# Seven products instead of eight for the up and gate projection of two segment groups

## The chip, the cores and the metric

One core of a Trainium2 chip runs the whole kernel. The metric is device time in microseconds (us): the median over several runs. The engines are PE (matrix multiply), DVE (vector), ACT (activation, scalar), POOL (GpSimd) and SP, which here only issues DMAs; each works off its own queue of instructions in order.

## The reference

One layer of a streaming encoder over 2192 tokens (8 requests of 16, 16 meta tokens, one prompt of 2048), width 1024. A first half mixes tokens (RWKV and mLSTM heads). The second half is a gated network with a causal convolution over three tokens:

```
D_MODEL = 1024
D_FF = 2816
FFN_CONV = 3
...
    x = x + jnp.concatenate([ya, yb], axis=-1).astype(x.dtype) @ w_out
    h2 = rmsnorm(x, norm_ffn)
    ug = h2 @ w_up
    u, fconv1 = causal_dwconv(ug[..., :D_FF], fconv0, ffn_conv_w, ffn_conv_b)
    x = x + (jax.nn.silu(u) * ug[..., D_FF:]) @ w_down
    return x, (shift1, S1, bconv1, C1, n1, m1, fconv1)
```

A last RMSNorm makes the outputs. All inputs and outputs are float32.

## The kernel before, in words

Activations lie with channels on the 128 partitions and tokens along the free axis. Tokens are cut into six segments, 0 to 5: segment 0 has 272, the others 384. A weight tile is 128 columns of a weight matrix against all eight blocks of 128 input channels.

Each factor of a large product is split into two parts that PE reads as fp32r: hi is a cast (ACT), lo is the source minus hi (DVE). `gemm` (L308 to L320) then runs three matmuls per block of 128 channels: hi by hi, hi by lo and lo by hi, all into one bank of PSUM. A product over 1024 channels is thus 24 matmuls.

`load_w` (L362 to L383) fetches a weight tile (512 KB) by SP's queue into a raw tile (2 of these), casts it on ACT (L374) and subtracts on DVE (L259), into one of four w tiles; a tile with a cache name is kept in DRAM in its two parts and comes again as 1 MB by POOL's queue. `split_acts` (L348 to L361) does the same for activations, two channel blocks (768 columns) at a time (L359, L360).

The first phase walks the six segments through the mixers, up to about 1880 us. At its end `ffn_acts` makes the split normed inputs (h2hi, h2lo) of segments 0 and 1.

The second phase is the gated network. The segments form three groups of two:

```
GROUPS = [[0, 1], [2, 3], [4, 5]]
CHUNKS = [(0, 5), (5, 10), (10, 14), (14, 18), (18, 22)]
```

For each group, the loop runs over chunks of f, a tile of 128 of the 2816 inner channels (22 in all). For each f, the u tile and the g tile of w_up are loaded, and `mm` computes u and g for both segments: 4 x 24 = 96 matmuls. Then u goes from PSUM to ub (ACT or DVE, L248 and L252), POOL puts the two tokens of the segment before at its front, DVE does the convolution in three steps (L1234, L1236 twice), ACT a tanh (L1238), DVE finishes the SiLU (L1239) and multiplies by g in PSUM (L1240); the result is split into gh (ACT, L1243) and gw (DVE and POOL in turn).

After each chunk, the down projection runs over eight output tiles d (`staggered`: the second segment one d behind the first), 3 matmuls per f, and DVE adds each bank to the residual x in SBUF (L1259). There are four residual tiles x2 (`mix`), so those of the next group load while a group still works. Ahead of the last down of a group, the inputs of the next group are made: `norm` scales x by the row's root mean square (broadcast by PE into ps_ch, L331; L1200) and splits it. For segment 5 the output projection of the mixers, `last_out`, is computed there too, ahead of the last down of the second group (L1189).

At the end of each group, squares are summed over channels (L1151 to L1155), over partitions on PE, the power is taken on POOL (L326, L327), PE broadcasts it, and DVE scales x for the output (L1266).

PSUM has eight banks under the tags gm (2), a, m, iv (2) and ch (2). A scheduler sets the order on each engine from the program's order and some places of preference (`ranked`); the engines' orders are then fixed. The pools cp, wp and big live over both phases.

Of the kernel before, what the change touches and what calls it, by code (L numbers as in the profile page):

```python
# [12 lines left out]
F32 = mybir.dt.float32  # L13
F32R = mybir.dt.float32r
AF = mybir.ActivationFunctionType
ALU = mybir.AluOpType
# [17 lines left out]
CHUNKS = [(0, 5), (5, 10), (10, 14), (14, 18), (18, 22)]  # L34
# [58 lines left out]
# Places in the scheduler's order, engines, PSUM rings and buffer counts of the stages.  # L93
# [118 lines left out]
def trunk_kernel(ctx: ExitStack, tc: tile.TileContext, A):  # L212
# [5 lines left out]
    def knob(name, default):  # L218
        """The first segment has its own choices, where there are any."""
# [4 lines left out]
    def rank(stage):  # L224
        """Instructions of a stage move by their knob's places in the scheduler's order of preference."""
# [40 lines left out]
    cst = cp.tile([128, CONST.shape[1]], F32, name="cst")  # L266
# [70 lines left out]
    def token_sums(pr, acc, n):  # L337
        """Sums over the channels, tokens on the partitions."""
# [9 lines left out]
    def split_acts(name, half, n, src=None, scale=None, raws=None):  # L348
        """float32r parts of an activation tile: src is loaded, scale(raw, k, j) fills or scales tile k in raw[:, j]."""
# [14 lines left out]
    def load_w(src, cache=None):  # L364
        """float32r parts of a weight tile; parts that come again are kept in DRAM."""
# [21 lines left out]
    def pt(tag, shape=(128, 512)):  # L387
        """A bank, in the shape asked for."""
# [6 lines left out]
    with ExitStack() as p1:  # L395
        pool = lambda n, b, **k: p1.enter_context(tc.tile_pool(name=n, bufs=b, **k))
        kp = pool("kp", 1)
# [53 lines left out]
        def build_h0():  # L451
            """The first segment's activations: squares are summed over the channels by ones on the tensor engine."""
# [50 lines left out]
        def shifted(w, h, s, ct, out):  # L503
            """Projected columns of tile ct, each mixed with the token before it."""
# [115 lines left out]
        def rwkv(u, s, ws, h, lo1, lo2):  # L620
# [157 lines left out]
            def chain():  # L778
# [4 lines left out]
                def sb(t, h):  # L783
                    """S' and the rank-one updates' left factors of head h."""
# [101 lines left out]
        def conv4(w, h, s, j, out):  # L886
            """Projected columns, causal conv of four taps and SiLU; j is the channel tile of q|k."""
# [142 lines left out]
        def out_proj(s, ds):  # L1030
            """Residual plus the projected mixers' output, kept in DRAM."""
# [23 lines left out]
        def ffn_acts(s):  # L1055
            """The normed input of the second half, for the segments that come first there."""
# [74 lines left out]
    with ExitStack() as p2:  # L1131
        pool = lambda n, b, **k: p2.enter_context(tc.tile_pool(name=n, bufs=b, **k))
        kp = pool("kp2", 1)
        accp = pool("acc", 4)
# [218 lines left out]
```

## Time and profile before

| | us |
|---|---|
| median of 3 runs | 3523.97 |
| lowest and highest run | 3508.24, 3531.34 |
| span of the profiled execution | 3507.6 |
| PE busy in this span | 3411.7 (97%) |
| DVE, ACT, POOL busy | 2146.4, 1152.2, 941.0 |

The profiled execution is one of its own; the page has its span, from the first to the last event on the core. The times of the runs are taken around the whole execution. A duration in the rows below is of this one execution; "busy" of a group of instructions counts overlapping ones once, so busy divided by the count is the distance between instructions that stand back to back, and the mean is that of a single one.

### The profile page before, as it was taken

How to read it: one execution, taken by the hardware profiler on the slowest of the kernel's cores; microseconds unless marked ns; L12 is line 12 of the kernel's file. 1: busy time of each engine (PE TensorE's matmuls, PEld its weight loads, DVE VectorE, ACT ScalarE, POOL GpSimd, SP SyncE). 2: the span in 40 equal slices, each digit the busy share in tenths (PEclk: the TensorE clock that was granted, in tenths of full speed). 3: DMA queues.
4: the chain of work that ended last, by engine and by line, in shares of the span. 5: the costliest groups of instructions: out<-in, count | busy, mean ns of one | idle time of the engine just before them, and what ended most of it. 6: DMA issues, size and time to landing. Idle time of an engine off the chain costs nothing.

```text
span 3507.6 us, 63114 instructions
## 1 busy us (share of the span) xinstructions
PE 3411.7 (97%) x24228; PEld 3123.6 (89%) x24228; DVE 2146.4 (61%) x5529; ACT 1152.2 (33%) x2826; POOL 941.0 (27%) x2294
## 2 busy tenths in 40 slices
PE   7999999999999999999989999999999999999998
PEld 6776888888888888888878999999999999999998
DVE  7777767666665776766665555574545447454544
ACT  5443444333433343343332222232222223222222
POOL 2532335434334444434421000021000012010002
PEclk9888999999999999999988999999999999999999
DMA  8753666455455545545523222232222233212221
GB/s 307 252 172 109 218 221 202 150 171 179 148 164 172 174 151 186 184 142 195 167 85 110 76 79 73 73 113 84 67 66 67 66 127 111 66 48 67 67 67 63
DMA packets 187565, 459.40 MB, mean 131 GB/s; under 512 B 68320, under 2 KB 111744, under 8 KB 156800
## 3 DMA queue, kind: packets, MB, share of 16 engines
q1 hardware_dynamic: 136648, 187.25, 18.0%
q0 software_dynamic: 28080, 204.48, 17.6%
q10 hardware_dynamic: 22536, 63.63, 4.8%
q8 instruction: 191, 3.13, 0.4%
q14 instruction: 110, 0.90, 0.1%
HBM read 381.68 MB, written 73.63 MB: 130 GB/s over the span
## 4 chain that ended last, share of the span: by engine, by line
PE 86%; DVE 6%; DMA 3%; ACT 2%; issue 1%; POOL 1%; ACTq 0%; SPq 0%; POOLq 0%; DVEq 0%
PE ps_gm L320 43%; PE ps_iv L320 11%; PE ps_a L320 10%; PE ps_m L320 5%; PE ps_iv L305 2%; PE ps_a L712 2%; PE ps_ch L826 1%; PE ps_ch L845 1%; PE ps_ch L839 1%; PE ps_iv L810 1%; PE ps_m L955 1%; DVE w L259 1%; DMA xt<-in_x_dram 1%; PE ps_a L305 1%; PE ps_m L972 1%
## 5 line engine op out<-in xcount | busy, mean ns | idle before, releaser
L320 PE MATMUL ps_gm<-hhi,w 128*128 128x384 f32 (+1 forms) x2976 | 813.1, 345 | 7.4 <-ACT w L374 2.2
L320 PE MATMUL ps_gm<-h2hi,w 128*128 128x384 f32 (+1 forms) x2816 | 701.1, 327 | 0.2 <-ACT ub L1221 0.2
L320 PEld LDWEIGHTS ps_gm<-hhi,w 128*128 128x128 f32 x2976 | 540.8, 193 | 30.2 <-issue 5.5
L320 PE MATMUL ps_gm<-hlo,w 128*128 128x384 f32 (+1 forms) x1488 | 502.2, 338 | 3.0 <-DVE hlo L360 3.0
L320 PEld LDWEIGHTS ps_gm<-h2hi,w 128*128 128x128 f32 x2816 | 500.0, 188 | 0.9 <-ACT ub L1221 0.5
L320 PE MATMUL ps_gm<-h2lo,w 128*128 128x384 f32 (+1 forms) x1408 | 459.9, 327 | 0.0
L374 ACT CAST w<-wraw 128x1024 fp32r<-128x1024 f32 (+2 forms) x291 | 259.4, 892 | 455.8 <-PE ps_iv L320 243.0
L320 PE MATMUL ps_iv<-gh,w 128*128 128x384 f32 (+1 forms) x1410 | 361.2, 330 | 0.0
L320 PE MATMUL ps_a<-h2hi,w 128*128 128x384 f32 (+1 forms) x1408 | 358.0, 327 | 0.0
L259 DVE TENSOR_TENSOR w<-wraw,w 128x1024 fp32r<-128x1024 f32 (+2 forms) x291 | 301.0, 1035 | 64.4 <-ACT w L374 60.4
L320 PEld LDWEIGHTS ps_gm<-hlo,w 128*128 128x128 f32 x1488 | 287.3, 193 | 9.5 <-DVE hlo L360 3.4
L320 PEld LDWEIGHTS ps_gm<-h2lo,w 128*128 128x128 f32 x1408 | 264.9, 188 | 0.0
L320 PEld LDWEIGHTS ps_iv<-gh,w 128*128 128x128 f32 x1410 | 252.5, 188 | 0.0
L320 PEld LDWEIGHTS ps_a<-h2hi,w 128*128 128x128 f32 x1408 | 251.0, 188 | 0.1
L320 PE MATMUL ps_iv<-gw,w 128*128 128x384 f32 (+1 forms) x705 | 232.6, 330 | 0.0
L320 PE MATMUL ps_a<-h2lo,w 128*128 128x384 f32 (+1 forms) x704 | 230.5, 327 | 0.0
L1238 ACT ACTIVATE fth<-ac 128x384 f32<-128x384 f32 (+1 forms) x132 | 67.2, 510 | 398.1 <-DVE ac L1236 388.7
L1231 POOL COPY h_f<-ub 128x2 f32<-128x2 f32 x88 | 16.4, 187 | 636.7 <-DVE ub L252 403.9
L320 PE MATMUL ps_m<-gh,w 128*128 128x384 f32 (+1 forms) x702 | 186.0, 330 | 0.0
L1259 DVE TENSOR_TENSOR x<-x,ps_iv 128x384 f32<-128x384 f32 (+1 forms) x160 | 85.3, 533 | 161.4 <-PE ps_iv L320 161.0
L1234 DVE TENSOR_SCALAR ac<-ub,d_fw,d_fb 128x384 f32<-128x384 f32 (+1 forms) x154 | 68.5, 457 | 182.8 <-ACT ub L248 157.1
L320 PE MATMUL ps_gm<-yhi,w 128*128 128x384 f32 (+1 forms) x640 | 168.3, 336 | 1.0 <-ACT yhi L359 0.7
(385 smaller groups left out, 6357.5 us busy)
## 6 DMA issues: line engine op xcount, KB each, us to landing
w<-wc POOLq DMA_DIRECT2D x155, 1024.0 KB, 5.4
wraw<-in_w_up_dram SPq DMA_DIRECT2D x132, 512.0 KB, 3.6
wc<-w ACTq DMA_DIRECT2D x31, 1024.0 KB, 6.5
wraw<-in_w_down_dram SPq DMA_DIRECT2D x72, 256.0 KB, 2.6
wraw<-in_w_in_dram SPq DMA_DIRECT2D x31, 512.0 KB, 5.9
wraw<-in_w_down_dram SPq DMA_DIRECT2D x48, 320.0 KB, 2.9
xraw<-in_xT_dram SPq DMA_DIRECT2D x36, 384.0 KB, 3.3
xt<-in_x_dram SPq DMA_DIRECT2D x15, 512.0 KB, 6.6
```

The source lines that it names most:

```text
L259: (V if e[turn[name] % len(e)] == "V" else G).tensor_tensor(out, a, b, op=op)
L305: T.matmul(out[h:h + 64], lhsT[h:h + 64], rhs[h:h + 64], start=start, stop=stop)
L320: T.matmul(ps, w, x, start=i == 0, stop=i == len(seq) - 1)
L374: S.copy(hi[:, :nk], raw[:, :nk])
L712: T.matmul(psS[hs, i, X], kb[hs, X, cl(c)], ar[hs, h, :, cl(c)], start=True, stop=True)
L810: T.matmul(pp[hs, i], TA[hs, 0, i], sb(SC[c][hs].unsqueeze(1), h)[:, 0], start=True, stop=True)
L826: T.matmul(pd[hs, :64], ar[:, h, x, cl(c)], vz[:, h], start=True, stop=x == 0)
L839: T.matmul(pz[hs, :64], kb2[:, h], vz[:, h], start=True, stop=True)
L845: T.matmul(py[hs, :64], sc[hs, 64:128], vz[hs, h], start=False, stop=True)
L1234: V.tensor_scalar(av, view(2), fwh[:, 44 + f:45 + f], fbh[:, f:f + 1], op0=ALU.mult, op1=ALU.add)
L1238: S.activation(th[:, :n], ac[:, :n], AF.Tanh)
L1259: V.tensor_tensor(X[s][:, d, :n], X[s][:, d, :n], p, op=ALU.add)
```

## The change

For the second and third group, u and g of both segments are computed as one product of 2 x 2 blocks by Strassen's scheme in Winograd's form. The left factor is [g; u] by two halves of the channels: A11 and A12 are the g tile's first and second four blocks, A21 and A22 those of the u tile. The right factor is the two halves of the channels (rows) by the two segments (columns): B11, B12, B21, B22. Seven products of half depth take the place of eight: 7 x 4 x 3 = 84 matmuls for 96. Its sums of weights are S1 = A21 + A22, S2 = S1 - A11, S3 = A11 - A21, S4 = A12 - S2; the sums of inputs are T1 to T4, made once per group (`ffn_parts`) with their hi and lo parts.

The products stay in three banks b1, b2, b3. Two are added in one bank by PE (start=False), and the sums that go to more than one output are taken by DVE from a bank read between two products (p1, u2, u3).

The first group is computed as before (`up_plain`). While it runs, it writes to DRAM: the two parts of each g tile (WG, 1 MB), of the second half of each u tile (WA, 0.5 MB), the raw sums S1 to S4 (WS, 1 MB; two sums on POOL, two on DVE) and the two parts of each down tile (WD). The other groups read these by SP's queue; the S tiles are split again on ACT and DVE in each group.

Further: the chunks are (0,3), (3,7), (7,11), (11,14), (14,17), (17,22); the down of a chunk stands behind the first f of the next chunk, and the finish of a group behind the first f of the next group. `last_out` moves into the first group, after the first chunk and one f more; its result is written to DRAM, like that of the other segments. There are two residual tiles instead of four, and the second phase has its own pool of weight tiles (wq: four w, three raw), which opens in the place of wp, a pool that now ends with the first phase. The convolution is an Identity on ACT with scale and bias, two steps on DVE, and a Silu on ACT. After the first group, `pinned` keeps the first matmul of each product in program order on PE.

The core of the diff:

```diff
-CHUNKS = [(0, 5), (5, 10), (10, 14), (14, 18), (18, 22)]
+CHUNKS = [(0, 3), (3, 7), (7, 11), (11, 14), (14, 17), (17, 22)]
...
-    wp = ctx.enter_context(tc.tile_pool(name="wp", bufs=1))
     big = ctx.enter_context(tc.tile_pool(name="big", bufs=2))
...
+    wp = p1.enter_context(tc.tile_pool(name="wp", bufs=1))
...
+        wq = pool("wq", 1)
-        accp = pool("acc", 4)
+        accp = pool("acc", 2)
...
+        quads = itertools.cycle([("gm", "iv", "a"), ("gm", "iv", "m")])
+        down_banks = itertools.cycle(("iv", "m", "iv", "a"))
...
+        def product(ps, w, x, start, stop):
+            for i, ((wh, wl), (xh, xl)) in enumerate(zip(w, x)):
+                for j, (l, r) in enumerate(((wh, xh), (wh, xl), (wl, xh))):
+                    ins = T.matmul(ps, l, r, start=start and i + j == 0, stop=stop and i == len(x) - 1 and j == 2, skip_group_check=not start)
+                    if pinned[0] and i + j == 0:
+                        tc.keep_in_program_order(ins)
...
+        def keep_sums(f, raw=None):
...
+            a11, a12, a21, a22 = raw["g"][:, 0:4], raw["g"][:, 4:8], raw["u"][:, 0:4], raw["u"][:, 4:8]
...
+            G.tensor_tensor(s1, a21, a22, op=ALU.add)
+            G.tensor_tensor(s3, a11, a21, op=ALU.subtract)
+            V.tensor_tensor(s2, s1, a11, op=ALU.subtract)
+            V.tensor_tensor(s4, a12, s2, op=ALU.subtract)
...
+        def conv(f, s, ub, ac):
...
+            for view, av in parts:
+                S.activation(av, view(2), AF.Identity, scale=PR("fw", 44 + f), bias=PR("fb", f))
+                for i in (1, 0):
+                    V.scalar_tensor_tensor(av, view(i), PR("fw", i * 22 + f), av, op0=ALU.mult, op1=ALU.add)
+            S.activation(ac[:, :n], ac[:, :n], AF.Silu)
...
+        def load_parts(f):
+            g = w_tile()
+            nc.sync.dma_start(f32(g), f32(WG[f][:]))
...
+            for i, names in enumerate((("S2", "S3"), ("S1", "S4"))):
+                raw = raw_tile()
+                nc.sync.dma_start(raw.rearrange("p (a k c) -> p a k c", a=2, c=128), WS[f][:, i])
+                t = w_tile()
+                split(t[:, 0], t[:, 1], raw.rearrange("p (k c) -> p k c", c=128))
...
+            a = w_tile()
+            nc.sync.dma_start(f32(a[:, :, 0:4]), f32(WA[f][:]))
...
+        def up_quad(f, segs, H, gl):
...
+            product(b1, W["A11"], H["B11"], True, True)
+            S.copy(p1, b1)
+            product(b2, W["S2"], H["T2"], True, True)
+            V.tensor_tensor(u2, b2, p1, op=ALU.add)
+            product(b1, W["A12"], H["B21"], False, True)
+            product(b2, W["S3"], H["T3"], False, True)
+            V.tensor_tensor(u3, b2, p1, op=ALU.add)
+            product(b3, W["S1"], H["T1"], True, True)
+            V.tensor_tensor(ub[1][:, 2:2 + n], b3, u3, op=ALU.add)
+            product(b2, W["A22"], H["T4"], False, True)
+            V.tensor_tensor(ub[0][:, 2:2 + n], b2, p1, op=ALU.add)
+            conv(f, segs[0], ub[0], ac[0])
+            V.tensor_tensor(ac[0], ac[0], b1, op=ALU.mult)
+            keep_gated(gl, f, segs[0], ac[0])
+            conv(f, segs[1], ub[1], ac[1])
+            product(b3, W["S4"], H["B22"], False, True)
+            V.tensor_tensor(u2, b3, u2, op=ALU.add)
+            V.tensor_tensor(ac[1], ac[1], u2, op=ALU.mult)
+            keep_gated(gl, f, segs[1], ac[1])
...
+        def ffn_parts(segs, rb):
...
+            for k in range(KD // 2):
...
+                    for i in range(2):
+                        V.scalar_tensor_tensor(r[:, i], r[:, i], PR("nf", j), rb[i], op0=ALU.mult, op1=ALU.mult)
...
+                pair(two[0], b2, ("B21", "B22"))
+                V.tensor_tensor(b1[:, 0], b1[:, 1], b1[:, 0], op=ALU.subtract)
+                V.tensor_tensor(b1[:, 1], b2[:, 1], b1[:, 1], op=ALU.subtract)
+                V.tensor_tensor(b2[:, 1], b2[:, 1], b1[:, 0], op=ALU.subtract)
+                pair(two[1], b1, ("T1", "T3"))
+                V.tensor_tensor(b2[:, 0], b2[:, 0], b2[:, 1], op=ALU.subtract)
+                pair(two[2], b2, ("T4", "T2"))
...
+        def group(g, segs, H, before):
...
+            for f0, f1 in CHUNKS:
+                gl = {}
+                for f in range(f0, f1):
+                    (up_quad if g else up_plain)(f, segs, H, gl)
+                    if before:
+                        before()
+                        before = None
+                    if due:
+                        if X is None:
+                            if g == 0:
+                                last_out()
+                            X = mix(segs)
+                        down(segs, X, *due, Q)
+                        due = None
+                due = gl, f0, f1
+                if g == 0 and f1 in (11, 14):
+                    keep_sums(f1 // 3 - 3)
+            if g + 1 < len(GROUPS):
+                rb = norm_banks(GROUPS[g + 1])
+            down(segs, X, *due, Q)
+            return rb, lambda: finish(segs, X, Q)
...
+            rb, after = group(0, GROUPS[0], H, None)
+        xp1 = p2.enter_context(tc.tile_pool(name="xp1", bufs=1))
+        H = ffn_parts(GROUPS[1], rb)
+        pinned[0] = True
+        rb, after = group(1, GROUPS[1], H, after)
+        H = ffn_parts(GROUPS[2], rb)
+        _, after = group(2, GROUPS[2], H, after)
+        after()
```

The first piece is PE's order inside an f of the second group: before, a part of one of its four products of 24 matmuls (h2hi and h2lo are the parts of the normed input, w a weight tile).

```order
L320 MATMUL ps_gm<-h2lo,w 128x384
L320 MATMUL ps_gm<-h2hi,w 128x384 x2
L320 MATMUL ps_gm<-h2lo,w 128x384
L320 MATMUL ps_gm<-h2hi,w 128x384 x2
L320 MATMUL ps_gm<-h2lo,w 128x384
L320 MATMUL ps_gm<-h2hi,w 128x384 x2
```

Now, the same engine and place: the first six of the seven products of an f, less a block of the first (h_283.. and hs hold the parts of the next inputs; gm, iv and a are b1, b2 and b3).

```order
L1186 MATMUL ps_gm<-h_28386,w 128x384 x3
L1186 MATMUL ps_gm<-h_28410,w 128x384 x3
L1186 MATMUL ps_gm<-h_28434,w 128x384 x3
L1186 MATMUL ps_iv<-hs,w 128x384 x12
L1186 MATMUL ps_gm<-h_28363,w 128x384 x3
L1186 MATMUL ps_gm<-h_28387,w 128x384 x3
L1186 MATMUL ps_gm<-h_28411,w 128x384 x3
L1186 MATMUL ps_gm<-h_28435,w 128x384 x3
L1186 MATMUL ps_iv<-hs,w 128x384 x12
L1186 MATMUL ps_a<-hs,w 128x384 x12
L1186 MATMUL ps_iv<-hs,w 128x384 x12
```

A product is 12 matmuls now, and every bank is written by a second product after it has been read.

The second piece is DVE's order in the last down of the first group, as changed: x_23850 and x_23852 are the residuals of segments 0 and 1, w from wr a down weight, and hraw and wr (L1368 on) the next group's inputs.

```order
L1410 TENSOR_TENSOR x_23850<-x_23850,ps_iv 128x272
L1410 TENSOR_TENSOR x_23852<-x_23852,ps_m 128x384
L1178 TENSOR_TENSOR w<-wr,w 128x640
L1368 SCALAR_TENSOR_TENSOR wr<-wr,par,ps_ch 128x384
L1410 TENSOR_TENSOR x_23850<-x_23850,ps_iv 128x272
L1368 SCALAR_TENSOR_TENSOR wr<-wr,par,ps_ch 128x384
L1178 TENSOR_TENSOR h_28386<-wr,h_28386 128x384
L1385 TENSOR_TENSOR wr<-wr 128x384
L1410 TENSOR_TENSOR x_23852<-x_23852,ps_iv 128x384
```

The inputs' work, which before stood ahead of the last down in the program, stands between the x adds of this down; the first scaling in a wr tile comes behind the fourth x add of segment 0 and the third of segment 1.

The third piece is DVE's order at the finish of the first group: before, where ub, ac and gw belong to the first f of the second group, and x_22936 and x_22939 are the residuals that are finished.

```order
L345 COPY tss<-ps_ch 16x1
L252 COPY ub<-ps_gm 128x384
L1234 TENSOR_SCALAR ac<-ub,d_fw,d_fb 128x384
L1236 SCALAR_TENSOR_TENSOR ac<-ub,d_fw,ac 128x384 x2
L1239 SCALAR_TENSOR_TENSOR ac<-fth,ac 128x384
L1266 SCALAR_TENSOR_TENSOR x_22936<-x_22936,par,ps_ch 128x272 x8
L345 COPY tss<-ps_ch 128x1 x3
L1240 TENSOR_TENSOR ac<-ac,ps_a 128x384
```

Now, at the same place: w from wr are the sums of weights of the first f, hs from wr the last parts of the inputs, and uu (L1329) is u2.

```order
L1455 SCALAR_TENSOR_TENSOR x_23850<-x_23850,par,ps_ch 128x272 x8
L1389 TENSOR_TENSOR wr<-wr 128x384
L1178 TENSOR_TENSOR w<-wr,w 128x1024
L1167 COPY tss<-ps_ch 128x1 x3
L1178 TENSOR_TENSOR w<-wr,w 128x1024
L1178 TENSOR_TENSOR hs<-wr,hs 128x768
L1455 SCALAR_TENSOR_TENSOR x_23852<-x_23852,par,ps_ch 128x384 x8
L1329 TENSOR_TENSOR uu<-ps_iv,p_28469 128x384
L1332 TENSOR_TENSOR uu<-ps_iv,p_28469 128x384
```

Both finishes now stand ahead of u2 of the first f, and the last split of the inputs stands between them.

## Rows read from the trace of the kernel before

**Rows 1.** The page: busy us of each engine; granted clock in 40 slices.

```profile
PE 3411.7 (97%) x24228; PEld 3123.6 (89%) x24228; DVE 2146.4 (61%) x5529; ACT 1152.2 (33%) x2826; POOL 941.0 (27%) x2294
...
PEclk9888999999999999999988999999999999999999
```

**Rows 2.** Stretches: length, PE, PEld, DVE, ACT, POOL busy, PEclk, DMA share, GB/s.

```profile
1800.00:1820.00 20.00, 19.30 (x150) 16.36 (x150) 14.76 (x37) 8.17 (x19) 1.22 (x3) 0.99 0.28 92
1820.00:1840.00 20.00, 16.69 (x122) 12.80 (x122) 10.37 (x39) 5.58 (x18) 5.41 (x10) 0.69 0.13 43
1840.00:1860.00 20.00, 19.92 (x173) 15.37 (x172) 10.05 (x43) 5.38 (x20) 0.00 (x0) 0.50 0.03 11
1860.00:1880.00 20.00, 14.06 (x71) 10.94 (x71) 12.01 (x44) 4.80 (x20) 6.21 (x13) 0.70 0.11 34
...
2400.00:2600.00 200.00, 200.00 (x1149) 200.00 (x1148) 93.02 (x147) 43.59 (x65) 14.44 (x36) 1.00 0.21 63
...
2360.00:2380.00 20.00, 20.00 (x121) 20.00 (x120) 15.42 (x26) 5.02 (x8) 2.11 (x5) 1.00 0.81 289
...
2860.00:2870.00 10.00, 10.00 (x60) 10.00 (x59) 7.20 (x13) 3.20 (x5) 1.81 (x5) 1.00 0.80 251
```

**Rows 3.** The chain, 2360 to 2420 us: start, length, what.

```profile
2380.97 8.32 PE ps_gm L320 x48
2389.29 4.16 PE ps_a L320 x24
```

**Rows 4.** Waits of PE, 2150 us to the end.

```profile
PE ps_ch L331 <- POOL rs L327: 6.8, 2, 5.2
```

**Rows 5.** Groups of DVE by form, 1950 us to the end.

```profile
L259 DVE TENSOR_TENSOR w<-wraw,w 128x1024 fp32r<-128x1024 f32 x122 | 149.2, 1223 | 29.6 <-ACT w L374 29.6
L1236 DVE SCALAR_TENSOR_TENSOR ac<-ub,d_fw,ac 128x384 f32<-128x384 f32 x210 | 130.7, 623 | 10.8
L1259 DVE TENSOR_TENSOR x<-x,ps_iv 128x384 f32<-128x384 f32 x133 | 73.5, 553 | 153.5 <-PE ps_iv L320 153.5
...
L259 DVE TENSOR_TENSOR w<-wraw,w 128x640 fp32r<-128x640 f32 x43 | 35.4, 824 | 5.3 <-ACT w L374 5.3
L259 DVE TENSOR_TENSOR gw<-ac,gh 128x384 fp32r<-128x384 f32 x44 | 24.5, 557 | 25.0 <-ACT gh L1243 25.0
L1266 DVE SCALAR_TENSOR_TENSOR x<-x,par,ps_ch 128x384 f32<-128x384 f32 x40 | 21.4, 607 | 5.4 <-PE ps_ch L331 5.3
...
L360 DVE TENSOR_TENSOR h2lo<-xraw,h2hi 128x768 fp32r<-128x768 f32 x16 | 15.6, 1003 | 0.3 <-ACT h2hi L359 0.2
L1200 DVE SCALAR_TENSOR_TENSOR xraw<-x,par,ps_ch 128x384 f32<-128x384 f32 x28 | 15.6, 607 | 0.0
...
L1259 DVE TENSOR_TENSOR x<-x,ps_iv 128x272 f32<-128x272 f32 x24 | 10.5, 436 | 5.8 <-PE ps_iv L320 5.4
...
L1266 DVE SCALAR_TENSOR_TENSOR x<-x,par,ps_ch 128x272 f32<-128x272 f32 x8 | 3.4, 493 | 0.5 <-PE ps_ch L331 0.5
```

**Rows 6.** Groups of ACT by form, 1950 us to the end.

```profile
L374 ACT CAST w<-wraw 128x1024 fp32r<-128x1024 f32 x122 | 128.4, 1053 | 174.9 <-PE ps_iv L320 102.5 <-PE ps_m L320 51.1 <-PE ps_gm L320 8.5
L1238 ACT ACTIVATE fth<-ac 128x384 f32<-128x384 f32 x105 | 55.2, 525 | 343.5 <-DVE ac L1236 338.7 <-DMA out_o_y_dram<-x 4.8
...
L248 ACT COPY ub<-ps_gm 128x384 f32<-128x384 f32 x36 | 17.4, 482 | 104.8 <-PE ps_gm L320 104.8
```

**Rows 7.** DMA issues of the page, and of 2100 to 3500 us: KB, us to landing.

```profile
w<-wc POOLq DMA_DIRECT2D x155, 1024.0 KB, 5.4
...
x<-in_xT_dram ACTq DMA_DIRECT2D x1, 1536.0 KB, 7.1
```

**Rows 8.** Timeline of DVE and POOL, 2398 to 2416 us: start, length, what.

```profile
2398.78 1.22 DVE L259 TENSOR_TENSOR w<-wraw,w 128x1024 fp32r<-128x1024 f32 x1
...
2399.49 1.39 POOL L259 TENSOR_TENSOR gw<-ac,gh 128x384 fp32r<-128x384 f32 x1 [5.16 <-ACT gh L1243]
2415.73 1.02 POOL L259 TENSOR_TENSOR gw<-ac,gh 128x384 fp32r<-128x384 f32 x1 [4.76 <-ACT gh L1243]
```

More of the change, by code (lines that the diff above doesn't have):

```diff
@@ new lines, in token_sums2, with wide @@
+        def token_sums2(pr, acc, n):
+            ss = cp.tile([128, 3], F32, name="tss", tag="tss", bufs=2)
+            if n % 128:
+                G.memset(ss, 1.0)
+            for i, (o, r) in enumerate(tok_tiles(n)):
+                T.matmul(pr[:r, i:i + 1], acc[:, o:o + r], one, start=True, stop=True)
+            for i, (o, r) in enumerate(tok_tiles(n)):
+                V.tensor_copy(ss[:r, i:i + 1], pr[:r, i:i + 1])
+            return ss
+        def wide(name, tag, w=NW):
+            return ep.tile([128, w], F32, name=name, tag=tag)
@@ new lines, in w_tile, with kparts, load_raw, raw0 @@
+        def w_tile():
+            return wq.tile([128, 2, KD, 128], F32R, name="w", tag="w", bufs=4)
+        def kparts(t, n=KD):
+            return [(t[:, 0, i], t[:, 1, i]) for i in range(n)]
+        WG, WA, WS, WD = {}, {}, {}, {}
+        def load_raw(f, new):
+            raw = {}
+            for n, t in (("u", f), ("g", NFF + f)):
+                raw[n] = new().rearrange("p (k c) -> p k c", c=128)
+                nc.sync.dma_start(raw[n], A["w_up"][t])
+            return raw
+        def raw0():
+            return xp0.tile([128, 1024], F32, name="wr0", tag="wr0", bufs=5)
@@ new lines, in down @@
+        def down(segs, X, gl, f0, f1, Q):
+            W = {}
+            for d, s in staggered(segs, 1):
+                n = SEGS[s][1]
+                if d not in W:
+                    W[d] = load_down(d, f0, f1)
+                p = (pt2("dn") if s < 2 else pt(next(down_banks), (128, NW)))[:, :n]
+                product(p, W[d], [gl[f, s] for f in range(f0, f1)], True, True)
+                V.tensor_tensor(X[s][:, d, :n], X[s][:, d, :n], p, op=ALU.add)
+                if f1 == NFF:
+                    square_sum(Q, s, X[s][:, d, :n], d, n)
@@ new lines, in last_out @@
+            c0, n = SEGS[s]
+            hi, lo = (accp.tile([128, KD, NW], F32R, name="y", tag="x2") for _ in range(2))
+            for k in range(0, KD, 2):
+                raw = raw_tile()[:, :2 * n].rearrange("p (k t) -> p k t", t=n)
+                nc.sync.dma_start(raw, yd[s][:, k:k + 2])
+                split(hi[:, k:k + 2], lo[:, k:k + 2], raw)
+            acc = wide("oacc", "ub", 388)[:, :n]
+            for d in range(KD):
+                w = w_tile()
+                nc.sync.dma_start(f32(w), f32(WC["o", d][:]))
+                p = pt(next(down_banks), (128, NW))
+                product(p, kparts(w), [(hi[:, k], lo[:, k]) for k in range(KD)], True, True)
+                xo = ep.tile([128, 2, NW], F32, name="xo", tag="uu")
+                nc.sync.dma_start(xo[:, 0], A["xT"][:, d, c0:c0 + n])
+                V.tensor_tensor(xo[:, 0], xo[:, 0], p, op=ALU.add)
+                nc.sync.dma_start(xd[s][:, d], xo[:, 0])
+                S.activation(xo[:, 1] if d else acc, xo[:, 0], AF.Square)
+                if d:
+                    G.tensor_tensor(acc, acc, xo[:, 1], op=ALU.add)
```

259 lines of the change are left out of this document (152 added, 107 removed).

## The prediction

> **What bounds the kernel now.** I read the page first, then the stretches, the chain, PE's waits, the groups by form, and the DMA landings. The page says that PE is busy for 97% of the span, DVE for 61%; the granted clock is below full in the first slices and just past the middle only [rows 1]. The stretches show why the part that is changed (up, gate and down projection, from about 1880 us on) is different from the first: in 200 us PE is busy for 200.00 at clock 1.00, with DVE at 93 and ACT at 44, and a stretch at an old group boundary, or one with DMA at 251 GB/s, is full too [rows 2]. The chain is nothing but matmuls there, 8.32 us for 48 and 4.16 for 24, so one of 384 columns costs 0.1733 us [rows 3]. From 2150 us to the end PE waits twice, 6.8 us in all, and both are at the last finish [rows 4]. So here a matmul less is 0.1733 us less, as long as nobody makes PE wait. In the stretches from 1800 to 1880, the end of the first phase, PE idles 10.0 us of 80 and the granted clock falls to 0.50, the lower level of 1.2 GHz [rows 2].
>
> **What is removed.** A pass over one f takes 96 matmuls of 384 columns in the second and third group; with seven products of 4 x 3 it takes 84. 2 groups x 22 f x 12 = 528 matmuls x 0.1733 = **91.5 us**. Down projection, the first group and the mixers keep theirs. An f's up part falls from 16.64 us to 14.56, a product takes 2.08.
>
> **What stands in the way inside a group.** Products share banks, so each second one waits for a sum on DVE: the fourth for u2, the sixth for u3, the seventh for the first segment's ub. By hand, with 0.55 for a sum, 0.62 for a conv step, 1.22 for a weight split and 0.56 for gw [rows 5], 1.05 for the cast and 0.48 for a copy from PSUM [rows 6], some 9 us of DVE stand against 14.56. The tightest is u2: behind the last gating of the f before it ends 1.0 us ahead of its product. Weights: an f now fetches 1 MB + three times 0.5 MB. The 1 MB tile's place is free after the third product (6.25 us) and is wanted at 14.56; a 1 MB tile lands in 5.4 us [rows 7], which leaves 2.9. So I take nothing per f. The bounds: a gain of none (PE is full already), and a loss of 0.3 us per f, if hops that I counted at under 0.1 us are twice as long: 13 us.
>
> The Silu in place of tanh and one multiply-add takes one DVE step (0.56) off each tile, and adds an Identity on ACT; tanh took 0.53 [rows 6], ACT is at 44 of 200 us: nothing. What hides it is PE's own work; without that cover it would be 0.5 us per tile.
>
> **The step from the first to the second group.** This is the largest cost. Last chunk's down is 8 x 15 x (0.123 + 0.173) = 35.5 us of PE (0.123 for 272 columns is an estimate, by columns from 0.173). The parts of the next inputs take raw tiles that the down weights hold too, so in DVE's order (second piece) three of the four rounds start only after 4 + 3 of the 16 x adds, 4 x 1.85 + 3 x 2.6 = 15.2 us into it. From there DVE has, up to the last split of parts: 12 scalings at 0.56 (15.6 us busy for 28), 12 differences and 3 splits at 0.56, 9 wide splits at 1.0, weights 0.8 + 2.4, 9 x adds 4.5, sums of squares and small copies, an estimate by columns, 1.6, the first finish 8 x 0.43 [rows 5]: 36.9 us, so 52 us. The second product, ready to run at 37.6, needs nearly all of it. Then the second segment's finish (8 x 0.535) is ahead of u2 in DVE's order (third piece), and the fourth product, due at 35.5 + 3 x 2.08 = 41.7, starts at 52.1 + 4.3 + 0.55 = 57.0: **15.3 us** of PE. Behind such a gap the clock is low for a while: after the thin stretch 1820 to 1840 the next 20 us were at 0.50 [rows 2]. The second and third product (4.2 us) fall in it: **+2 us**. Bounds: 0, if DVE gets ahead in gaps that I can't see, and 30, if rounds also wait for their loads.
>
> **From the second to the third group.** All four rounds fit better, as down lasts 41.6 us. What is left is late by 1.6 us (the last gated tile), about 2.3 (sums, rs on POOL, broadcast: twice 6.8 us in all were waited for at the last finish, with nothing beside it [rows 4]; here a product lies beside it) and 2.2 (the finish, 4.3 on DVE, ahead of u2, less one product): **6 us, +1** for the clock. Bounds 0 and 13. The last finish keeps its shape: nothing.
>
> **The first group.** Its own matmuls are the same. It now also stores 2.5 MB per f: at 14.2 us per f some 250 GB/s with what it reads. A stretch with 251 GB/s kept PE full [rows 2], so nothing, up to 10 us if it doesn't. The output projection of the last segment moves here, before the first down, and its activations lie in the only two residual tiles; so the residuals load after it, 7.1 us for the large one [rows 7], of which three banks of down products (3 x 1.2 us) cover half: **3.5 us**. Sums on POOL and DVE (two each of 512 columns, under 1.9 us apiece by POOL's 384-wide rows [rows 8]) lie beside 14.2 us: nothing. Small starts and loads: **2 us**.
>
> **The seam of the phases.** In both kernels 72 matmuls of the first f stand in PE's order before the mixers end. The new weight ring opens only when the whole old pool is free, so they come about 10 us later and fill less of the 10.0 us that PE idles there. Bounds −5 (they leave the stretch at half clock) and +8; I take **+4**.
>
> **Sum.** −91.5 + 17.3 + 7 + 3.5 + 2 + 4 = −57.7. On the profiled execution's span of 3507.6 that is 3449.9; the median of the runs, 3523.97, lies 16.4 above this span, and I carry the difference over: **3466 us**, −1.6%.
>
> **Rivals.**
> *The steps are hidden.* DVE is at half load, and old boundaries show no loss [rows 2]; against it, the finish and x adds now share DVE with 33 us of new parts. Then −91.5 + about 5: 3437.
> *DVE gives way to POOL.* Where a split on DVE and gw on POOL overlapped, DVE took its usual 1.22 and POOL 1.39 instead of 1.02 [rows 8], so POOL gave way. Were it DVE that waits out the whole gw, u2 would be 0 to 0.6 us late behind its 1.0 us of slack, 28 us at most over 44 f: 3466 + 14 = 3480 in the middle. By the Trainium skill (SBUF — State Buffer, Who interferes with whom) a DVE instruction with two SBUF inputs contends with a GpSimd one that reads SBUF, and whoever issues first keeps the port while the other fully blocks; the rows agree where DVE issued first, and no row above has the other order.
> *The seams are worse.* Rounds wait for loads (30 instead of 15.3), the seam of phases costs 8, the first group 10: −91.5 + 32 + 10 + 17 + 8 = −24, 3500, no measurable change.
> *The weight stream decides (slower side).* All four tiles of an f stand in one queue. If neighbours slow the 1 MB tile from 5.4 to twice that, 10.8, it is 10.8 − 8.3 = 2.5 us late in each f: +110, 3466 + 110 = 3576. It decides from (91.5 − 34) / 44 = 1.3 us per f on. For it: 0.81 of the DMA engines were busy in a stretch at a boundary [rows 2]. Against: the mean would be near 180 GB/s, and PE stayed full at 251.
> *It does not do what it says.* The order has 12 matmuls per product and seven products; only PE's waits could hide the gain, which are the cases above.
>
> **How the numbers follow.** The forecast has 0.56; hidden steps 0.12; DVE giving way 0.10; worse seams 0.14; the weight stream 0.08. A difference of about 1% (35 us) is what a measurement of this kernel can tell from no change: faster is below 3488.7, slower above 3559. The forecast lies below but for a little; of DVE giving way a good half; worse seams are "same"; the weight stream is slower, but for a little: faster 0.74, same 0.19, slower 0.07. The range leaves out half of the hidden steps below, and the weight stream above: 3430 to 3512.
>
> **What would show it.** PE full at clock 1.00 inside groups, with pieces of about 2.08 us per product; the f near 14.6 us. Two holes, at the first and second step, of 15 and 6 us, in which PE waits for DVE (weight split, parts, u2), the clock below 1.00 behind them. A short wait for an x add after the output projection. It is wrong if PE waits in each f for ACT's cast or for a DMA (weight stream), for u2 (DVE), or if the two holes are missing or twice as long.

## The result and the profile after

The changed kernel took 3463.98 us (median of 4 runs, 3459.44 to 3470.22), the kernel before 3518.79 (4 runs, 3508.24 to 3531.34): a ratio of 0.9846, 95% interval 0.9818 to 0.9874, 54.8 us less. The forecast was 3466, 57.7 less than the 3523.97 then known for the kernel before. The profiled execution's span is 3457.7, 49.9 under that of before.

The page of the changed kernel, busy us of the engines, answers to [rows 1]:

```profile
PE 3320.1 (96%) x23700; PEld 3031.0 (88%) x23700; DVE 2154.1 (62%) x5475; ACT 1197.5 (35%) x2936; POOL 1066.1 (31%) x2407
```

PE is busy for 91.6 us less, and yet the span is only 49.9 shorter: some 42 us of new idle time have come. PE's share of the span is 96%, where it was 97%.

Stretches of the changed kernel (length, PE, PEld, DVE, ACT, POOL busy, PEclk, DMA share, GB/s), to be read against [rows 2]:

```profile
1880.00:1890.00 10.00, 3.32 (x17) 3.10 (x16) 10.00 (x15) 3.78 (x6) 5.19 (x7) 0.78 0.75 271
1900.00:3400.00 1500.00, 1473.54 (x8839) 1467.80 (x8838) 829.87 (x1371) 441.74 (x755) 295.47 (x489) 0.99 0.57 197
2390.00:2400.00 10.00, 1.82 (x12) 1.40 (x11) 8.45 (x16) 4.33 (x6) 5.95 (x3) 0.71 0.19 59
2400.00:2410.00 10.00, 6.90 (x24) 5.62 (x24) 7.16 (x15) 1.78 (x2) 2.96 (x3) 0.50 0.90 277
2410.00:2420.00 10.00, 8.74 (x53) 8.46 (x53) 5.50 (x11) 1.05 (x1) 0.00 (x0) 0.94 0.97 355
2500.00:2600.00 100.00, 100.00 (x575) 100.00 (x574) 46.97 (x77) 25.27 (x39) 11.94 (x23) 1.00 0.47 163
2920.00:2930.00 10.00, 8.31 (x42) 8.07 (x41) 5.73 (x12) 2.88 (x5) 2.99 (x4) 0.83 0.72 220
```

The same 1500 us of the kernel before:

```profile
1900.00:3400.00 1500.00, 1500.00 (x9032) 1499.81 (x9031) 794.31 (x1364) 386.62 (x627) 173.50 (x372) 1.00 0.25 78
```

Inside a group (2500 to 2600) PE is full at clock 1.00. From 1900 to 3400 it idles 26.5 us, where before it idled nothing, and half of that (13.0) lies between 2380 and 2420, the step from the first to the second group. In the 10 us from 2400, behind most of the hole, the granted clock is 0.50, the lower level of 1.2 GHz. From 1880 to 1890, at the seam of the phases, DVE is busy for all 10 us and PE for 3.3. DMA moves 197 GB/s in these 1500 us, 78 before.

What PE waited for from 1850 us to the end (line waited for: us in total, times, longest), against [rows 4]:

```profile
PE ps_ch L1158 <- POOL rs L329: 15.7, 5, 6.8
PE ps_gm L1186 <- DVE ac L1294: 7.6, 2, 6.7
PE ps_gm L1186 <- ACT ub L1290: 4.5, 1, 4.5
...
PE ps_iv L1186 <- DVE w L1178: 2.8, 1, 2.8
...
PE ps_iv L1186 <- ACT gh L1177: 2.2, 2, 1.3
PE ps_iv L1186 <- DVE x L1410: 2.0, 1, 2.0
PE ps_gm L1186 <- ACT p L1327: 1.7, 1, 1.7
PE ps_iv L1186 <- POOL gw L1178: 1.7, 2, 1.0
PE ps_gm L1186 <- DMA w<-wg: 1.4, 1, 1.4
```

The largest is the broadcast of rs in the finish: 6.8 us of it at the first step. The 6.7 us for L1294 and the 4.5 for L1290 are the seam of the phases, where PE waited 0.2 us for the first products' banks before. The weight stream (wg) is missed once, for 1.4 us, and no row repeats 44 times: there is no wait per f.

The chain inside a group, 2500 to 2560 us (start, length, what):

```profile
2510.78 2.08 PE ps_iv L1186 x12
2512.87 2.12 PE ps_gm L1186 x12
2514.99 2.08 PE ps_iv L1186 x12
2517.07 2.08 PE ps_m L1186 x12
2519.15 2.08 PE ps_iv L1186 x12
2521.23 2.12 PE ps_m L1186 x12
2523.36 2.12 PE ps_gm L1186 x12
```

A product is 2.08 or 2.12 us; the seven rows add up to 14.68, one f.

How far the mixers' end lies from the end of the span tells the second phase apart from the first. The mixers' last matmul in the timeline of PE, before and then after:

```profile
1875.46 0.90 PE L1018 MATMUL ps_m<-cst,nd 128*128 128x128 f32 x3 [2.46 <-DVE nd L1016]
```

```profile
1866.06 0.90 PE L1019 MATMUL ps_m<-cst,nd 128*128 128x128 f32 x3 [2.46 <-DVE nd L1017]
```

From there to the end it is 3507.6 - 1875.46 = 1632.1 us before and 3457.7 - 1866.06 = 1591.6 after: 40.5 less. I call this distance the rest, and use it for all that follows.

The other 9.4 of the 49.9 lie ahead of this matmul. Where the mixers' end falls differs by more than that between executions of one kernel (the run of the kernel before, below), but one stretch ahead of it repeats. It runs from one pair of matmuls of the mixers (ps_m from vt and kw) to the next, before and then after:

```profile
1835.35:1860.65 25.30, 24.78 (x212) 19.04 (x212) 12.98 (x57) 6.91 (x27) 1.55 (x4) 0.50 0.06 19
```

```profile
1835.09:1850.92 15.83, 14.69 (x190) 11.21 (x187) 11.43 (x55) 6.02 (x23) 1.16 (x3) 1.00 0.06 19
```

It takes 25.3 us at a granted clock of 0.50 in both executions of the kernel before, and 15.83 us at 1.00 in the changed kernel and in each of its seven variants below. 24 of its 211 small matmuls stand ahead of it after the change, so not all of the difference is gained. Over a longer piece, from an earlier pair of these matmuls (at 1702.45 before, 1700.85 after) to the mixers' end, it is 173.0 and 176.9 us in the two executions before, and 163.2 to 168.2 in the other eight: 9.6 less in the mean. So the change makes the mixers' end come some 10 us earlier, and this gain stands outside of the rest. The 72 matmuls of the first f, which in both kernels lie ahead of the stretch, begin at 1815.64 instead of 1804.90 and end 2 us ahead of it instead of 12. That they keep the clock up is not shown by a run of its own.

### The profile page after: what moved, and what is told of

Same layout as the page of the kernel before. It is cut to its first block, busy times and chain, and to the rows that moved or that the text cites. A ratio compares the mean times of both kernels' runs of the same rounds, so it can differ in the third digit from the quotient of the medians.

```text
span 3457.7 us, 62687 instructions
## 1 busy us (share of the span) xinstructions
PE 3320.1 (96%) x23700; PEld 3031.0 (88%) x23700; DVE 2154.1 (62%) x5475; ACT 1197.5 (35%) x2936; POOL 1066.1 (31%) x2407
## 5 line engine op out<-in xcount | busy, mean ns | idle before, releaser
L1177 ACT CAST w<-wr 128x1024 fp32r<-128x1024 f32 (+3 forms) x180 | 166.7, 926 | 609.0 <-PE ps_iv L1186 509.7
L1186 PE MATMUL ps_iv<-hs,w 128*128 128x384 f32 x1584 | 299.5, 337 | 3.5 <-DVE w L1178 2.8
L1186 PEld LDWEIGHTS ps_iv<-hs,w 128*128 128x128 f32 x1584 | 279.1, 189 | 4.3 <-DVE w L1178 3.3
L1178 DVE TENSOR_TENSOR w<-wr,w 128x1024 fp32r<-128x1024 f32 (+3 forms) x180 | 202.9, 1127 | 102.9 <-ACT w L1177 99.7
L1186 PE MATMUL ps_gm<-h2hi,w 128*128 128x272 f32 (+1 forms) x944 | 220.1, 318 | 12.2 <-DVE ac L1294 7.6
L1186 PE MATMUL ps_gm<-h,w 128*128 128x384 f32 x1056 | 202.0, 341 | 3.1 <-ACT p L1327 1.7
L1268 DVE SCALAR_TENSOR_TENSOR ac<-ub,par,ac 128x384 f32<-128x384 f32 (+2 forms) x308 | 174.1, 602 | 43.4 <-ACT ac L1266 35.0
L1186 PEld LDWEIGHTS ps_gm<-h,w 128*128 128x128 f32 x1056 | 187.9, 188 | 3.5 <-ACT p L1327 1.8
L1186 PEld LDWEIGHTS ps_gm<-h2hi,w 128*128 128x128 f32 x944 | 164.9, 193 | 13.6 <-DVE ac L1294 8.1
L322 PE MATMUL ps_gm<-yhi,w 128*128 128x384 f32 (+1 forms) x640 | 168.2, 336 | 1.1 <-ACT yhi L361 0.7
L372 POOL DMA_DIRECT2D w<-wc x155 | 92.2, 595 | 221.0 <-PE ps_gm L322 174.1
```

Of the source, the lines that this page charges most:

```text
L322: T.matmul(ps, w, x, start=i == 0, stop=i == len(seq) - 1)
L372: nc.gpsimd.dma_start(w, WC[cache][:])
L1177: S.copy(hi, src)
L1178: eng.tensor_tensor(lo, src, f32(hi), op=ALU.subtract)
L1186: ins = T.matmul(ps, l, r, start=start and i + j == 0, stop=stop and i == len(x) - 1 and j == 2, skip_group_check=not start)
L1268: V.scalar_tensor_tensor(av, view(i), PR("fw", i * 22 + f), av, op0=ALU.mult, op1=ALU.add)
```

## The experiments

Up to the last one, each experiment is one execution, so only its rest and the stretches of its trace are compared with the changed kernel's.

**The finish behind the second f.** The edit: the finish of a group is called one f later, and the matmuls of its sums are kept in program order.

```diff
-                    if before:
+                    if before and f == 1:
                         before()
...
+                if pinned[0]:
+                    tc.keep_in_program_order(ins)
```

> The changed kernel with the finish of a group moved from behind the first f of the next group to behind the second, held there by PE's order. In the changed kernel PE stands still 13.0 us at the step from the first to the second group. Theory (DVE's backlog: parts, weight split and finish in one queue): the 6.8 us wait for the rs broadcast goes, the second product waits only for the last split of parts, u2 no longer stands behind the finish; PE idles about 8 us there, and the clock comes back sooner: the span falls from 3457.7 by 5 to 8 us, to about 3451. Rival (the parts alone set the hole): the hole stays at 12 to 13 us and only its releaser changes. At the second step, the 2.0 us wait for rs goes as well.

Its span was 3473.7, its rest 3473.7 - 1867.45 = 1606.2: 14.6 us more, where 5 to 8 less were expected. PE's timeline at the step shows both halves of it:

```profile
2400.37 1.01 PE L1188 MATMUL ps_iv<-hs,w 128*128 128x384 f32 x2 [7.29 <-ACT w L1179]
2402.37 3.57 PE L1188 MATMUL ps_iv<-hs,w 128*128 128x384 f32 x10 [0.99 <-DVE w L1180]
...
2435.86 1.75 PE L1158 MATMUL ps_ch<-cst,rs 128*128 128x128 f32 x6 [3.31 <-POOL rs L329]
...
2442.71 1.65 PE L1158 MATMUL ps_ch<-cst,rs 128*128 128x128 f32 x6 [3.73 <-POOL rs L329]
2444.02 4.19 PE L1188 MATMUL ps_gm<-h,w 128*128 128x384 f32 x12
```

The hole at the step is 7.29 + 0.99 = 8.3 us, as the theory of the backlog had it. But the finish now stands in PE's queue with nothing between its sums and its broadcast: 3.3 and 3.7 us of waiting, and a product that takes nearly twice its time behind them (4.19 for 2.28), at a granted clock of 0.66 from 2430 to 2450. The expectation left that out. At the second step, where it had the 2.0 us for rs go, they became 8.9 (3.2 and 5.7). Over the rest PE idles 6.7 us more than in the changed kernel, and its busy time is 7.9 longer, at the lower clock behind the waits. So the time is a miss, the hole at the first step is a hit, and the last experiment but one parts the two.

**The scaling of the sums on DVE.**

```diff
-                rs_pow(token_sums2(pt2("rb"), Q[s], n), rs)
+                ss = token_sums2(pt2("rb"), Q[s], n)
+                V.tensor_scalar(rs, ss, 1.0 / D, EPS, op0=ALU.mult, op1=ALU.add)
+                G.tensor_tensor(rs, rs, mhalf[:, :3], op=ALU.pow)
```

> The changed kernel with the scaling of the 128x3 sums (the tensor_scalar ahead of the power, in the finish only) on DVE instead of POOL; the power stays on POOL. In the changed kernel that tensor_scalar took 3.98 us on POOL at the first step, against 0.20 elsewhere. Theory A (POOL is held off while DVE runs instructions with two SBUF inputs back to back): now the power, the next instruction of POOL, is drawn out in its place, to about 4 us from 0.87, PE's wait for rs stays near 6.8 us and the hole near 13 us. Theory B (the tensor_scalar itself was slow on POOL at that moment): the power takes 0.9, PE's wait falls by about 4 us to 3, and the hole to about 9 us.

Rest 1593.3, that of the changed kernel within 2. Theory A holds. First POOL's timeline of the changed kernel at the step, then that of this run, with PE's wait:

```profile
2394.53 3.98 POOL L328 TENSOR_SCALAR rs<-tss 128x3 f32<-128x3 f32 x1 [3.44 <-DVE tss L1167]
2398.59 0.87 POOL L329 TENSOR_TENSOR rs<-rs,mhalf 128x3 f32<-128x3 f32 x1
2406.56 1.97 POOL L328 TENSOR_SCALAR rs<-tss 128x3 f32<-128x3 f32 x1 [7.09 <-DVE tss L1167]
```

```profile
2394.20 4.47 POOL L1453 TENSOR_TENSOR rs<-rs,mhalf 128x3 f32<-128x3 f32 x1 [4.83 <-DVE rs L1452]
```

```profile
2398.72 1.76 PE L1158 MATMUL ps_ch<-cst,rs 128*128 128x128 f32 x6 [7.74 <-POOL rs L1453]
```

Whichever 128x3 instruction comes first on POOL there is drawn out to 4 us, PE waits 7.7 us for it, and the hole is 12.5 (13.0 in the changed kernel), not the 9 of theory B. DVE's timeline of the changed kernel says what it was waiting for:

```profile
2394.37 0.94 DVE L1178 TENSOR_TENSOR hs<-hraw,hs 128x768 fp32r<-128x768 f32 x1
2395.23 0.54 DVE L1386 TENSOR_TENSOR wr<-wr 128x384 f32<-128x384 f32 x1
2395.70 0.94 DVE L1178 TENSOR_TENSOR h<-wr,h 128x768 fp32r<-128x768 f32 x1
...
2397.51 0.94 DVE L1178 TENSOR_TENSOR hs<-wr,hs 128x768 fp32r<-128x768 f32 x1
2401.31 3.36 DVE L1455 SCALAR_TENSOR_TENSOR x<-x,par,ps_ch 128x272 f32<-128x272 f32 x8 [2.87 <-PE ps_ch L1158]
```

From 2394.37 to 2398.45 DVE runs two-input instructions without a gap, and POOL's ends at 2398.51, as soon as DVE stops. The one at 2406.56, which took 1.97 us, does the same: two splits on DVE end at 2408.47, POOL's at 2408.53. Behind the first, DVE idles 2.87 us for the broadcast that waited for POOL.

**Two sums of weights later.** f = 2 and 3 are left out of the sums made while they are loaded, and made at the ends of later chunks; those of 0 and 1 come one chunk earlier by it.

```diff
-            if f >= 2:
+            if f >= 4:
                 keep_sums(f, raw)
...
-                if g == 0 and f1 in (11, 14):
-                    keep_sums(f1 // 3 - 3)
+                if g == 0 and f1 in (7, 11, 14, 17):
+                    keep_sums((7, 11, 14, 17).index(f1))
```

> The changed kernel with the sums of weights of f = 2 and 3 made at the end of later chunks (as those of 0 and 1 are), not while the mixers end. In the changed kernel PE waits 6.7 us for the gating of the first f on DVE there, and its 768-wide split took 3.17 us on DVE against 0.95 elsewhere. Theory (POOL's two sums and DVE's splits hold each other off at the seam, and DVE's queue is late by that): the wait of 6.7 us falls to under 2, and the 768-wide splits there to under 2 us; the end of the fourth f moves ahead by about 5 us, the span by 3 to 6. Rival (the seam is late because weights come late into the new ring): the wait for the gating stays above 5 us, or a wait for weights takes its place, and the span stays within 2 us of 3457.7.

The wait of 6.7 us for L1294 is gone from PE's list. From the mixers' last matmul to the end of the fourth f it took 1928.61 - 1874.26 = 54.4 us instead of 1929.89 - 1866.06 = 63.8, a gain of 9.5 where about 5 were expected. This repeats: the five variants without the edit have 63.3 to 63.9, the last run, which has it too, 55.7. The rest fell by only 5.5, to 1586.1, since the first step idled 15.3 us for 13.0 in this execution and the clock stood at 0.97 instead of 1.00 from 1900 to 2000. The span (3460.4) says nothing, as the mixers ended 8.2 us later in this execution. First the 768-wide splits and the convolution's steps of 128 columns on DVE in the changed kernel, then two of POOL's sums there, then DVE's in this run:

```profile
1872.59 3.90 DVE L1178 TENSOR_TENSOR y<-wr,y 128x768 fp32r<-128x768 f32 x2 [1.47 <-ACT y L1177]
...
1877.88 3.43 DVE L1268 SCALAR_TENSOR_TENSOR ac<-ub,par,ac 128x128 f32<-128x128 f32 x2
...
1887.74 3.17 DVE L1178 TENSOR_TENSOR y<-wr,y 128x768 fp32r<-128x768 f32 x1
```

```profile
1872.43 1.28 POOL L1216 TENSOR_TENSOR ws<-wr 128x512 f32<-128x512 f32 x1
...
1887.85 1.28 POOL L1216 TENSOR_TENSOR ws<-wr 128x512 f32<-128x512 f32 x1
```

```profile
1880.94 2.69 DVE L1178 TENSOR_TENSOR y<-wr,y 128x768 fp32r<-128x768 f32 x3 [1.46 <-ACT y L1177]
1883.55 1.70 DVE L1268 SCALAR_TENSOR_TENSOR ac<-ub,par,ac 128x128 f32<-128x128 f32 x5
...
1890.37 1.78 DVE L1178 TENSOR_TENSOR y<-wr,y 128x768 fp32r<-128x768 f32 x1
```

Two splits took 3.90 us beside two sums on POOL, and three took 2.69 without; two convolution steps took 3.43 beside two sums, and five took 1.70 without. The split at 1887.74 took 3.17 beside a sum and a gw on POOL, and 1.78 in this run, beside a gw. Here it is DVE that waits: POOL's sums take 1.28 us, where their median is 1.30. So the sums explain 9.5 of the seam's 14 us. The other part stays in all variants: PE waits 4.4 to 4.7 us at the seam for ACT's copy of the first product to ub, and ACT, idle for 7.7 us, waits for the mixers' last store (yd<-yo). Tiles of the second phase that open only behind the first are a reason for it that no run tested.

**An eighth product.**

```diff
             product(b2, W["S3"], H["T3"], False, True)
+            product(b2, W["S3"], H["T3"], False, True)
             V.tensor_tensor(u3, b2, p1, op=ALU.add)
```

> The changed kernel with an eighth product in each f of the second and third group: the fourth (S3 by T3) is added a second time, 12 more matmuls, so that u is not the reference's; all loads, splits and sums stay. Theory (PE alone sets the time within a group): the span rises by 44 x 2.1 = 92 us to about 3550, no matmul less than one of these is hidden. Rival (PE waits in each f for DVE or weights, by a little each time): it rises by less than 80 us, since a part of the added time lies in those waits.

Rest 1683.0 against 1591.6: 91.4 us for 528 matmuls more, 92 were expected. (The span rose by 106.9; 15.6 of that lie ahead of the mixers' end.) A matmul added in these groups costs its full 0.173 us, so PE alone sets the time inside a group.

**The g tile twice.**

```diff
             nc.sync.dma_start(f32(g), f32(WG[f][:]))
+            nc.sync.dma_start(f32(g), f32(WG[f][:]))
```

> The changed kernel with the 1 MB tile of the two g parts fetched twice into the same place for each f of the second and third group (the second fetch brings what the first did). It measures the slack of the weight stream, which the prediction put at 2.9 us for this tile (8.3 us from free place to use, 5.4 us to land). Theory (slack of about 3 us): two fetches one after the other take 9.6 to 10.8 us, so PE waits 1.3 to 2.5 us in each f for the tile, and the span rises by 57 to 110 us. Rival (the stream has far more slack, as tiles are fetched long before): under 20 us. Rival (it has none, and was hiding losses already): over 150 us.

Rest 1676.5, 84.9 us more, within the theory's 57 to 110. A piece of its chain:

```profile
2616.26 2.14 PE ps_gm L1186 x12
...
2618.41 4.83 DMA w<-wg
2623.25 4.74 DMA w<-wg
...
2628.04 2.35 PE ps_gm L1186 x12
```

The first fetch starts when the third product has given the tile's place free, two fetches take 9.6 us, and in the middle of the second group (2440 to 2870) the next f begins 1.5 us late in the mean (22.4 us of PE's waits in 15). Over both groups it is 66.8 us in 37 waits, one of them 11.7; the other 18 of the 84.9 are for the most part PE's busy time at a lower clock, such as 0.93 from 3000 to 3100. One fetch of 4.8 thus has about 9.6 - 1.5 - 4.8 = 3.3 us of slack, near the 2.9 that the prediction worked with.

**The kernel before, again.**

> The kernel before, unchanged, profiled once more, to see how far the mixers' end (its last matmul, the product for nd, at 1875.46 us in its first profile, 1866.06 in that of the changed kernel, and 1863.5 to 1881.6 in those of its variants) moves from one execution to the next. Theory (it moves by itself): it lies anywhere from 1863 to 1882, and the time from there to the end is 1632 us within 2. Rival (the change moved it): it lies within 2 us of 1875.46.

Its mixers' last matmul began at 1885.08, 9.6 us later than in the first profile, and the rest was 3518.3 - 1885.08 = 1633.2, against 1632.1. So the first phase moves by itself by some 10 us (this one lies 3 us outside of the range that was given), and the rest repeats within about 1 us. The theory is not the whole of it: the stretch of the mixers shown above takes 25.3 us here too, against 15.83 with the change, so some 10 us of where their end falls belong to the change.

**The finish taken apart.**

```diff
+            def sums():
...
+            def scale(s):
...
+            return {0: sums, 1: lambda: scale(segs[0]), 2: lambda: scale(segs[1])}
...
+                    if before and f in before:
+                        before[f]()
```

> The changed kernel with the finish taken apart: sums over partitions and the power behind the first f of the next group, the broadcast and scaling of its first segment behind the second f, of its second segment behind the third, held there by PE's order, the scaling at low preference on DVE. Theory (the hole at the first step is DVE's backlog of parts, 8 us, and the finish's own chain adds 5, which stood in PE's queue with nothing beside it when the whole finish was put behind the second f): the hole at the step is 8 to 9 us as there, and the rs waits of 3.3 and 3.7 us and the slow stretch behind them go; from the mixers' last matmul to the end it takes 1591.6 - 8 = about 1583 us. Rival (the finish costs PE what it costs wherever it stands): 1590 or more.

Rest 1578.2, 13.4 less than the changed kernel, where 8 were expected. PE's timeline at the step:

```profile
2406.32 1.01 PE L1190 MATMUL ps_iv<-hs,w 128*128 128x384 f32 x2 [7.32 <-ACT w L1181]
2408.32 3.57 PE L1190 MATMUL ps_iv<-hs,w 128*128 128x384 f32 x10 [0.99 <-DVE w L1182]
```

The hole is 8.3 us once more (8.5 with two small waits), and DVE's chain there has no gap above 0.7 us from 2382 to 2408: this part is DVE's backlog. The waits for rs are gone from the groups, and the rival falls. Of the 13.4 us, 10.9 are PE's idle time: 4.5 at the first step, 4.5 at the second (from 2900 to 3000 PE is busy for 98.83 us, where it was 94.25 in the changed kernel) and 2.5 behind 3380 us, at the last finish; 0.6 more came in the first group. The expected 8 had counted the first experiment's waits of 3.3 and 3.7, which the changed kernel doesn't have there, and neither the second step nor the last finish.

**All three together.** The finish taken apart, the sums of f = 2 and 3 later, and the gw of the last f on DVE.

```diff
-            split(gh[:, :n], gw[:, :n], ac[:, :n], (V, G)[(f + s) % 2])
+            split(gh[:, :n], gw[:, :n], ac[:, :n], V if f == NFF - 1 else (V, G)[(f + s) % 2])
```

> The finish taken apart as above, the sums of weights of f = 2 and 3 made later, and the gw of the last f always on DVE (POOL's share of it ended 1 us after PE wanted it, at the end of two groups). By the theory the three add up, as they lie at different places: 8 from the finish, 5 (measured alone: 1586.1 from the mixers' last matmul instead of 1591.6) and 2, so 1577 from the mixers' last matmul to the end and a median near 3464 - 15 = 3449. Rival (what is saved at one place is waited for at the next): 3460 or more.

3447.82 us (median of 5 runs, 3438.35 to 3453.57; before 3520.74 on that chip): a ratio of 0.9787, interval 0.9765 to 0.9810, which doesn't overlap with the changed kernel's 0.9818 to 0.9874. The median expected was 3449. Rest 1566.7, 24.9 less than the changed kernel's, and 10 below the 1577 expected; the sum of the parts measured alone is 13.4 + 5.5 and about 2. The edit of the sums gives more here than alone, as its own execution lost 4 us of the seam's 9.5 elsewhere. The stretch answers to the one above:

```profile
1900.00:3400.00 1500.00, 1483.34 (x8929) 1478.76 (x8928) 839.36 (x1381) 445.63 (x762) 295.73 (x498) 1.00 0.58 201
```

PE idles 16.7 us there instead of 26.5; half of it is the hole of DVE's backlog at the first step, which no edit removed.

## Why the prediction was right

The forecast of 3466 met 3464, and the difference of 57.7 met 54.8; that the two times lie closer than the two differences is luck, as the median of the kernel before fell from 3523.97 to 3518.79 with its fourth run. By its steps:

| term | forecast | measured |
|---|---|---|
| 528 matmuls less | -91.5 | 44 x (16.64 - 14.68) = -86 |
| seam of the phases | +4 | +14.3 from the mixers' end to that of the fourth f (63.83 us, 49.55 before), and -9.6 in the mixers ahead of it |
| output projection, residuals | +3.5 | 2.9 |
| rest of the first group | +2 | 1.0 |
| first step | +15.3, +2 for the clock | 13.0, about 4.5 |
| second step, with its last gated tile | +6, +1 | 5.7 + 1.9, about 1.4 |
| last gated tile of the third group | none | 2.0 |

Without what lies ahead of the mixers' end, the measured terms give -86 + 14.3 + 26.5 of waits + 5.9 of clock = -39.3, and the rest fell by 40.5. With it they give -49, as the profiled span (-49.9); the medians differ by 54.8, and the 6 us between lie within what the first phase moves by itself.

*The saving.* Right, and shown by the eighth product: PE is the bound inside a group. It was 5 us too large because three of the seven products take 2.12 us, not 2.08 (12 matmuls at the 0.1733 of [rows 3]). These three read the parts of the inputs themselves, not of their sums T; but with the finish taken apart they take 2.08 to 2.09 and two others 2.11, so it isn't the tiles alone, and why is open.

*No wait per f.* Right. DVE ends u2 in time, and the weight stream's slack of 2.9 us is about what the second fetch measured (3.3). The rival of the slower side had a price near to what was measured (2.5 us per f for a tile that takes twice as long; the second fetch cost 84.9 / 44 = 1.9) but not the cause: with 163 GB/s a 1 MB tile still lands in 4.8 us.

*The first step.* Right in size, and partly right in its mechanism. The hole is DVE's queue, as forecast. But the prediction had the second product wait for the last parts, and then u2 for the finish; in the trace PE stood for 6.8 us at the broadcast of the first finish, which is in PE's own queue ahead of the second product's end. The experiments part it: 8.5 us are the backlog of parts and the weight split, the other 4.5 the finish's chain. In that chain POOL's 128x3 instruction is held off by DVE for 3.8 us, which no step of the prediction had. That 15.3 met 13.0 with another chain is in part luck. The clock cost 4.5 us (PE's busy time in the three stretches from 2390 to 2420, times what the granted clock lacked: 0.5 + 3.5 + 0.5), not 2, since sums and broadcasts ran at 0.50 as well as products.

*The second step.* Right in size (7.6 with the gated tile, 6 forecast without the clock); the waits are the last gated tile (0.9 + 1.0), rs (2.0), the copy of the first product on ACT (1.7) and one late g tile (1.4, not forecast).

*The seam.* Its net is near the forecast (14.3 - 9.6 = 4.7 against 4), and neither half is. The prediction let the 72 matmuls come about 10 us later, which they do, and gave at most 5 us for their leaving the stretch at half clock; measured, it is the mixers' own work that leaves it, and their end comes 9.6 us earlier. Behind the mixers' end 14.3 are lost. The step that failed is the first group's "Sums on POOL and DVE ... lie beside 14.2 us: nothing": beside the y splits and the convolution at the seam they cost 9.5 us, as their removal showed. The prediction gave "DVE gives way to POOL" a chance of 0.10 and looked for it in each f of the later groups. There it did not come (a 1024-wide split on DVE took 1.24 us there in the mean, 1.22 in [rows 5]); it came at the seam, and in the other direction at the first step. By the Trainium skill (SBUF — State Buffer, Who interferes with whom), whoever issues first keeps the port for its instruction. Two cases agree: POOL's sum began at 1872.43, ahead of DVE's split at 1872.59, and DVE waited; DVE's split began at 2394.37, ahead of POOL's step at 2394.53, and POOL waited. The split at 1887.74 does not: by the profile it began 0.11 us ahead of POOL's sum, and yet DVE waited. And POOL at the first step was held off over a run of six instructions of DVE, not one.

*What helped.* At the seam two errors of some 10 us cancel. The other terms don't: 5 us less saved, 2 at the third group's end, 2 more for the second step and 3 for the clock, against 4 less in the first step's hole and the first group. By its terms the change gives 49 us, as the two profiled spans do (49.9), 8 or 9 short of the forecast; that the medians come within 3 us of the forecast is in part luck.

## What to carry to other kernels

Where one engine is full, price a change of its work at the interval in the chain, and then look for the places where its queue stands behind another engine's burst: here some 33 us of one-off DVE work at a group's boundary, by the prediction's count. A short chain that crosses three engines (sums, power, broadcast) belongs in PE's queue in pieces, with a product's worth of other work between each; moved as a whole, one f later, it waited longer. And to judge an edit in the second half of a program, measure from a fixed instruction in its middle: the part ahead of it lay up to 20 us apart between executions here, and the edits were worth 2 to 15. But look at that part too, from one of its instructions to another: here it held some 10 us of the change's gain.

## What was not expected of the hardware

A POOL instruction on 128x3 elements took 3.98 us instead of 0.20, and with that step moved away the next took 4.47 instead of 0.87: POOL was held off until DVE's run of two-input instructions ended. In the other direction two 768-wide splits on DVE took 3.90 us instead of about 1.8 beside two sums of 512 columns on POOL. A stretch of the mixers, which the change was not meant to touch, took 15.83 us at a granted clock of 1.00 instead of 25.3 at 0.50, with other matmuls ahead of it and 24 of 211 small ones fewer in it. And products of the same 12 matmuls took from 2.08 to 2.12 us, for no reason that the runs show.
